# Two-layer hybrid decoder step: all feed-forward-in blocks by seven half-size products, even tiles first

## The chip, the cores and the metric

One Trainium2 chip, one core of it. The metric is the device time of one execution of the whole program in microseconds (us), as the median over the runs.

## The reference, cut to what matters

```python
def trunk_layer(x, pos, lw, states, front_pad, chunk, attend):
    m, new_states = hybrid_mixer(rmsnorm(x, lw['g_pre_mix']), ...)   # [...] @ lw['w_out'] at its end
    x = x + rmsnorm(m, lw['g_post_mix'])
    gate, up = jnp.split(rmsnorm(x, lw['g_pre_ffn']) @ lw['w_ffn_in'], 2, axis=-1)
    x = x + rmsnorm((jax.nn.silu(gate) * up) @ lw['w_ffn_out'], lw['g_post_ffn'])
    return x, new_states
```

There are two layers, 1104 tokens (9 token tiles: 8 of 128 and tile 8 of 80), a model width of 1024 and a feed-forward width of 2816. All data is float32.

## The kernel before, in words

Every float32 operand of a large product is split into two float16 halves (high and low), and a product is three float16 matmuls (high by high, high by low, low by high). Weights come from HBM as float32 into one of two `raw` buffers, ScalarE (ACT) writes the high half, VectorE (DVE) the low half; this is a split, and its result is a slab `wsp` in one of three `w` slots, three `w2` slots, or a `big` buffer.

The body is a set of Python generators, among which a planner (class `Plan`, line 116) picks the next by its own clocks; what it picks sets the order of the instructions on each engine, and each engine works through its own queue in that order. The places that matter here all lie in `dense` and what it starts:

- **Output projection** (lines 934 to 969). For each token tile i, two matmul groups (`hf`) of 24 matmuls of 512 columns into a PSUM bank `pd` (two banks take turns), evicted into `m`. For tiles 6 to 8 (`part`) seven of the eight contraction steps were done earlier and stored in `od`; here 3 matmuls per half are left, and DVE adds them to the loaded `m`. Tile i needs the outputs of the token mixers for tile i, the last of which is the delta-rule chain of head 3.
- **The norms of a tile** (`out_post`, line 2034, with `post_norm` and `norm_t`): a sum of squares on ACT, a scale and a power on GpSimd (POOL), a multiply with the gain and an add on DVE, a second sum of squares, scale, power and multiply, then eight 128x128 transposes on TensorE (PE) through the banks `ps_tr` and `ps_ch`, and their split into `xn2`. `xn2` keeps even tiles in its first half of columns and odd tiles in the second; tile 8 lies half in each.
- **Feed-forward in** (lines 973 to 1069), 22 column blocks c. Blocks 0 to 2 (`NPL`) are plain: gate and up for all 1104 tokens, first the columns of tiles 0 to 3 for all three blocks (k = 0), then the rest (k = 1). Blocks 3 to 21 are a Strassen scheme: tokens, contraction and gate/up are halved, and seven products of 24 matmul pairs of 256 and 296 columns replace the eight half-size products of a plain block.
- **The operands of the seven products** (`combos`, line 791): products 1 and 2 read the even half of `xn2` (a11, a12); products 5, 6 and 3 read sums `st`, product 7 a sum that overwrites a21 in `xn2`. Per group q of two tiles DVE, POOL and ACT work out the sums; `S1` marks `st`, `S3` the overwrite. The overwrite waits for the end of the plain blocks. DVE and POOL share the two-operand elementwise work by `tt` (line 308).
- **Weight loads** (`order_loads`, line 702; `loader`, `load7`): the queue order is the order of `want`. A Strassen block takes two loads of 512 KB and makes four slabs from 7 splits of 512 columns, with four sums on DVE or POOL.

Of the kernel before, what the change touches and what calls it, by code (L numbers as in the profile page):

```python
# [30 lines left out]
HS = 0.5 * DS * DS * XS  # L31
NPL = 3
NPT = 3
# [251 lines left out]
def build(tc, A, depth=DEPTH):  # L285
# [129 lines left out]
    def load7(my, key, src):  # L415
# [50 lines left out]
    def loader():  # L466
        while True:
# [13 lines left out]
            if spare:  # L481
                yield room(1)
                hold()
                raw = big([128, 1024], F32, "rawg")[:, :n]
                dma(raw, src)
            elif src is not None:
                wfree["raw"] -= 1
                raw = rawp.tile([128, 1024], F32, tag="raw", name="raw")[:, :n]
                dma(raw, src)
            if key[0] == "w2" and key[2] == 0:  # L490
# [211 lines left out]
    def order_loads(L):  # L702
# [87 lines left out]

    def combos(L, it, own):

# [38 lines left out]
        for q in own:  # L831
            f, g = temps(q)
            a11, a21 = part(xv[0, 0], q), part(xv[1, 0], q)
            yield (("S1", l, q),)
            tt(g, a11[:, :, 1], a21[:, :, 1], SUB)
            tt(f, a11[:, :, 0], a21[:, :, 0], SUB)
            tt(f, f, g, ADD)
            yield None
            put(a21, f)
            mark(("S3", l, q))  # L840
            yield None
        free()


    def dense():
        for L in LY[:depth]:
# [92 lines left out]
            mark(("gains", l))  # L939
            for i in range(NT):  # L940
                C = tsz(i)
# [6 lines left out]
                if not L.first:  # L948
# [22 lines left out]
            P.add(0, when([("xn2", l, i) for i in range(NT)], lambda: free(2)))  # L971

            yield (("ffn", l),)
            for k, c in [(k, c) for k in range(2) for c in range(NPL)]:
                wk = [("wi", l, c, z) for z in range(2)]
                if k == 0 and c % 2 == 0:
                    yield room(2)
                    hold(2)
                    hid_new(L)
                for h in range(2):  # L980
                    yield tuple(wk) + tuple(("xn2", l, i) for i in (4 * k + h, 4 * k + h + 2, 8 * k))
                    g0, gn = h * HT + CH[k][0], CH[k][1]
                    pgu = []
                    for gu in range(2):
                        p = pd(True)[:, :gn]
                        pgu.append(p)
                        for kt in range(8):
                            o = gu * 512 + kt % 4 * 128
                            w = slab[wk[kt // 4]][0]
                            mm3(p, w[:, 0, o:o + 128], w[:, 1, o:o + 128], L.xn2[:, kt, 0, g0:g0 + gn],  # L990
                                L.xn2[:, kt, 1, g0:g0 + gn], kt == 0, kt == 7)
                            yield NOW
                    a = abp.tile([128, 384], F32, tag="a", name="a")[:, :gn]
                    act(a, pgu[0], AF.Tanh, scale=DS * 0.5)
                    stt(a, a, 1.0, pgu[0], ADD, MUL)
                    for o, c0, cn in hid_out(L, c, h, k):
                        stt(o, a[:, c0:c0 + cn], HS, pgu[1][:, c0:c0 + cn], MUL, MUL)
                    yield NOW
                if k:
                    for w in wk:  # L1000
                        drop(w)
                    mark(("hid", l, c))
                if c == NPL - 1:
                    mark(("plain", l, k))

            yield room(1)
            hold()
            U = big([128, 2, HT], F32, "U")
            xv = L.xn2.rearrange("p (b k) z (s c) -> s b p k z c", b=2, s=2)
            ops = {1: xv[0, 0], 2: xv[0, 1], 3: L.st[:, 2], 4: xv[1, 1], 5: L.st[:, 0], 6: L.st[:, 1], 7: xv[1, 0]}  # L1010
            turn = 0
            for c in range(NPL, NF):
                if c % 2 == 0:
                    yield room(2)
                    hold(2)
                    hid_new(L)
                for n, (sl, o) in ((1, (0, 0)), (2, (0, 1)), (6, (1, 0)), (5, (1, 1)), (7, (2, 0)), (3, (2, 1)),
                                   (4, (3, 0))):
                    yield (("wi", l, c, sl),) + tuple(({6: "S1", 7: "S3"}[n], l, q) for q in range(5) if n > 5)
# [3 lines left out]
                    turn += 1  # L1023
                    for kt in range(4):
                        wh, wl = (w[:, z * 512 + kt * 128:z * 512 + kt * 128 + 128] for z in range(2))
                        x = ops[n][:, kt]
                        for z in range(2):
                            for q, (c0, cn) in zip(p, CH):
                                T.matmul(q[:, :cn], lhsT=wh, rhs=x[:, z, c0:c0 + cn], start=kt + z == 0, stop=False)
                        for q, (c0, cn) in zip(p, CH):  # L1030
                            T.matmul(q[:, :cn], lhsT=wl, rhs=x[:, 0, c0:c0 + cn], start=False, stop=kt == 3)
                        if kt < 3:
                            yield NOW
                    if o or sl == 3:
                        drop(("wi", l, c, sl))
                    for k, (q, (c0, cn)) in enumerate(zip(p, CH)):
# [1110 lines left out]
    for L in LY[:depth]:  # L2147
# [147 lines left out]
```

## Time and profile before

| | |
|---|---|
| median of 3 runs | 2858.16 us (2857.57 to 2859.92) |
| the profiled execution's own time | 2859.83 us |
| its span in the profile | 2858.0 us |
| PE busy in the span | 2730.1 us (96%) |
| DVE, ACT, POOL busy | 1938.0, 1287.5, 820.8 us |
| granted TensorE clock, mean | 0.984 |

Busy time of an engine is the sum of its instructions; PE is busy nearly all the time, so what counts is where it is not, and what it does there. A row of the timeline gives an instruction's start, its length, its engine, what it writes and reads, and in brackets how long its engine had been idle and which engine released it. Times are us from the span's start; layer 0's output projection and feed-forward-in begin at some 670, layer 1's at some 2083.

### The profile page before, as it was taken

The numbers are of one execution on the slowest core, as the hardware profiler recorded it, in microseconds if no ns is written. First come the engines' busy times: TensorE is split into PE (matmuls) and PEld (weight loads), VectorE is DVE, ScalarE is ACT, GpSimd is POOL, SyncE is SP. The second block draws the span as 40 slices with busy tenths as digits, with TensorE's granted clock in tenths as the row PEclk, the third lists the DMA queues.
The fourth block names the chain that finished last, engine by engine and source line by source line (L and its number), as shares of the span: only waits on it lengthen the run. The fifth ranks groups of instructions, "written<-read, shape, count | busy, mean of one in ns | idle before, by whom it ended". The sixth has DMA issues, their size and how long they took to land. (4 is left out here: it accounts for less than half of the span.)

```text
span 2858.0 us, 50012 instructions
## 1 busy us (share of the span) xinstructions
PE 2730.1 (96%) x19662; PEld 1907.6 (67%) x19662; DVE 1938.0 (68%) x3614; ACT 1287.5 (45%) x3015; POOL 820.8 (29%) x1124
## 2 busy tenths in 40 slices
PE   7999998999799999999999999999988999999998
PEld 4767676764588888744458676776646888887443
DVE  6467667655757776768875776666457667676778
ACT  5435456654423333433544455655543333333344
POOL 3205423313543333200260062233136232331002
PEclk9999999999899999999999999999999999999999
DMA  5011100132301111233340211001222111113324
GB/s 194 29 63 47 48 31 32 39 106 90 110 31 60 53 53 60 93 115 99 123 153 19 65 48 47 30 33 50 94 97 95 45 59 46 60 53 104 114 100 149
DMA packets 74092, 209.79 MB, mean 73 GB/s; under 512 B 13360, under 2 KB 24816, under 8 KB 73824
## 3 DMA queue, kind: packets, MB, share of 16 engines
q1 hardware_dynamic: 73856, 206.59, 22.0%
q8 instruction: 154, 2.52, 0.4%
q14 instruction: 82, 0.67, 0.1%
HBM read 175.49 MB, written 33.04 MB: 73 GB/s over the span
## 5 line engine op out<-in xcount | busy, mean ns | idle before, releaser
L215 PEld LDWEIGHTS <-wsp 128*128 128x128 f16 x10704 | 1044.4, 99 | 306.3 <-issue 14.6
L215 PE MATMUL pd<-xn,wsp 128*128 128x336 f16 (+3 forms) x4512 | 740.7, 311 | 3.4 <-DVE a L215 3.2
L215 DVE SCALAR_TENSOR_TENSOR wsp<-raw,wsp 128x512 f16<-128x512 f32 (+2 forms) x390 | 377.4, 977 | 184.1 <-ACT wsp L215 181.3
L215 ACT ACTIVATE wsp<-raw 128x512 f16<-128x512 f32 (+2 forms) x390 | 287.4, 749 | 367.3 <-DVE raw L215 106.5
L215 PEld LDWEIGHTS <-hsp 128*128 128x128 f16 x1848 | 180.9, 98 | 222.9 <-DVE hsp L215 4.3
L215 PE MATMUL pd<-wsp,hsp 128*128 128x512 f16 x924 | 224.5, 381 | 3.8 <-DVE hsp L215 1.9
L215 PE MATMUL ps_o<-wsp,hsp 128*128 128x512 f16 x924 | 222.5, 379 | 0.0
L215 PE MATMUL pd<-wsp,mixed 128*128 128x512 f16 (+1 forms) x864 | 212.6, 385 | 7.3 <-DVE m L215 7.3
L215 POOL TENSOR_SCALAR rqy<-ss 128x1 f32<-128x1 f32 (+1 forms) x72 | 65.5, 910 | 528.1 <-ACT jk L215 390.9
L215 DVE SCALAR_TENSOR_TENSOR u<-R,lp_cw,u 128x512 f32<-128x512 f32 x216 | 180.3, 870 | 11.3 <-ACT u L215 10.3
L215 ACT ACTIVATE hsp<-hid 128x512 f16<-128x512 f32 x154 | 89.9, 619 | 176.4 <-PE ps_o L215 143.8
L215 POOL TENSOR_TENSOR raw<-raw 128x512 f32<-128x512 f32 x74 | 95.6, 1293 | 241.9 <-DVE raw L215 212.6
L215 PE MATMUL ps_o<-xn,wsp 128*128 128x256 f16 (+1 forms) x1296 | 163.7, 284 | 0.0
L215 PE MATMUL pd<-wsp,xn 128*128 128x512 f16 (+3 forms) x864 | 156.0, 331 | 3.5 <-ACT wsp L215 1.7
L215 PE MATMUL ps_inv<-xn,wsp 128*128 128x256 f16 (+1 forms) x1248 | 154.0, 281 | 0.8 <-DVE a L215 0.8
L215 POOL TENSOR_TENSOR U<-U,hid 128x256 f32<-128x256 f32 (+1 forms) x114 | 80.3, 732 | 239.4 <-ACT hid L215 239.4
L215 PEld LDWEIGHTS <-mixed 128*128 128x128 f16 (+1 forms) x864 | 84.6, 101 | 84.3 <-issue 13.6
L215 DVE TENSOR_TENSOR hsp<-hid,hsp 128x512 f16<-128x512 f32 x154 | 101.2, 684 | 40.8 <-ACT hsp L215 40.8
L215 PEld LDWEIGHTS <-xn 128*128 128x128 f16 (+1 forms) x864 | 86.3, 101 | 51.1 <-issue 3.3
L215 PE MATMUL ps_ch<-xn,wsp 128*128 128x296 f16 x456 | 109.2, 289 | 0.0
L215 PE MATMUL ps_tr<-xn,wsp 128*128 128x256 f16 x456 | 108.6, 273 | 0.0
L215 DVE TENSOR_TENSOR W<-ps_inv,c 128x512 f16<-128x512 f32 (+1 forms) x120 | 71.0, 595 | 47.8 <-PE ps_inv L215 46.9
(498 smaller groups left out, 4790.9 us busy)
## 6 DMA issues: line engine op xcount, KB each, us to landing
raw<-wfi SPq DMA_DIRECT2D x88, 512.0 KB, 3.5
raw<-wfo SPq DMA_DIRECT2D x50, 512.0 KB, 3.6
raw<-wf SPq DMA_DIRECT2D x44, 512.0 KB, 3.3
xd<-xt SPq DMA_DIRECT2D x24, 512.0 KB, 2.9
xt<-xd SPq DMA_DIRECT2D x24, 512.0 KB, 4.7
rawg<-wfo SPq DMA_DIRECT2D x20, 512.0 KB, 4.3
xt<-x SPq DMA_DIRECT2D x16, 512.0 KB, 4.6
raw<-wo SPq DMA_DIRECT2D x16, 512.0 KB, 3.4
```

The source lines that it names most:

```text
L215: r = f(*a, **kw)
```

## The change

- `NPL` goes. All 22 blocks take the seven products. For the first four (`NPRE`) products 1 and 2 are done ahead of everything else (the "pre" products), as they read the even half alone, and are kept in the block's output buffers `hid`; after these the remaining five products of blocks 0 to 3 follow, then blocks 4 to 21 as before.
- The pre products have weights of their own: four loads `wj` of 512 KB, each a slab of 1024 columns. Blocks 0 to 3 load their full weights again afterwards, and leave out two of the seven splits.
- Output projection goes through the tiles in the order 0, 6, 8, 2, 4, 7, 1, 3, 5 (`OUT_SEQ`).
- `combos` takes the groups in the order 4, 3, 0, 1, 2, marks `S1` after the two sums that products 5 and 6 read, and does the other two at once, without a wait for plain blocks.

```diff
-NPL = 3
+NPRE = 4
+OUT_SEQ = (0, 6, 8, 2, 4, 7, 1, 3, 5)
...
         for k in range(4):
+            if k == 0 and key[2] < NPRE:
+                yield lambda: split[0] == my
+                tt(a, b, a, SUB)
+                continue
...
+        for c in range(NPRE):
+            want(("wj", l, c), A["wfi"][l, 2 * c:2 * c + 2, :, 0:4, :].rearrange("z p a b -> p z (a b)"), 1024, "f")
         for c in range(NF):
-            src = [A["wfi"][l, 2 * c + z].rearrange("p a b -> p (a b)") for z in range(2)]
-            if c < NPL:
-                for z in range(2):
-                    want(("wi", l, c, z), src[z], 1024, "f")
-            else:
-                want(("wi", l, c), src, 1024, "s")
+            want(("wi", l, c), [A["wfi"][l, 2 * c + z].rearrange("p a b -> p (a b)") for z in range(2)], 1024, "s")
...
-            tt(f, a12[:, :, 0], g, SUB)
-            tt(f, f, a12[:, :, 1], ADD)
-            yield None
-            put(part(L.st[:, 2], q), f)
             mark(("S1", l, q))
             yield None
-        if NPL:
-            yield (("plain", l, 0), ("plain", l, 1))
...
+            for o, a in ((a21, a22), (part(L.st[:, 2], q), a12)):
+                tt(f, a[:, :, 0], g, SUB)
+                tt(f, f, a[:, :, 1], ADD)
+                yield None
+                put(o, f)
+                yield None
             mark(("S3", l, q))
...
-            for i in range(NT):
+            for i in OUT_SEQ:
...
-            for k, c in [(k, c) for k in range(2) for c in range(NPL)]:
...
+            for c in range(NPRE):
...
+                for n in range(2):
+                    yield (("wj", l, c),) + tuple(("xn2", l, i) for i in (0, 2, 4, 6, 8))
+                    p = [pd(True) for _ in range(2)]
+                    yield from half(p, slab[("wj", l, c)][0].rearrange("p z a -> p (z a)"), n * 512, 1024, xv[0, n])
+                    for k, (q, (c0, cn)) in enumerate(zip(p, CH)):
+                        b1 = hid_out(L, c, 0, k)[0][0]
+                        for o, o0, on in hid_out(L, c, 1, k):
+                            if n == 0:
+                                act(o, q[:, o0:o0 + on])
+                            else:
+                                V.tensor_tensor(b1[:, o0:o0 + on], q[:, o0:o0 + on], o, op=ADD)
+                        if n:
+                            gate(b1, cn)
+                    yield NOW
+                drop(("wj", l, c))
...
-            for c in range(NPL, NF):
+            for c in range(NF):
...
-                                   (4, (3, 0))):
+                                   (4, (3, 0)))[0 if c >= NPRE else 2:]:
...
-        it = iter(range(5))
-        P.add(2, combos(L, it, (0, 2, 4)))
-        P.add(2, combos(L, it, (1, 3)))
+        it = iter((4, 3, 0, 1, 2))
+        P.add(2, combos(L, it))
+        P.add(2, combos(L, it))
```

Three places in layer 0 show how the instructions move. In the names below `m2_` and `xt_` are one tile's rows in output projection and its norms, `wsp_` a slab, `raw_` its loaded weights, `rqy_` what POOL's power gives, `pd_` a PSUM bank.

The first is DVE at the start of output projection, when tile 0's products are done (tile 0 is `m2_7804`). Before:

```order
L215 TENSOR_TENSOR m2_7804<-m2_7804,gpo_7466 128x1024
L215 SCALAR_TENSOR_TENSOR mixed_7594<-g__7788,nwd_355,mixed_7594 128x80
L215 SCALAR_TENSOR_TENSOR xt_7805<-m2_7804,rqy_7880,xt_7805 128x1024
L215 SCALAR_TENSOR_TENSOR wsp_7807<-raw_7073,wsp_7807 128x1024
L215 SCALAR_TENSOR_TENSOR wsp_7812<-raw_7155,wsp_7812 128x1024
L215 SCALAR_TENSOR_TENSOR m2_7804<-xt_7805,rqy_7887,gpf_7468 128x1024
```

With the change (tile 6 is `m2_7874`, tile 8 `m2_7916`):

```order
L216 TENSOR_TENSOR m2_7804<-m2_7804,gpo_7466 128x1024
L216 SCALAR_TENSOR_TENSOR m2_7874<-pd_7911,m2_7874 128x512
L216 SCALAR_TENSOR_TENSOR wsp_7807<-raw_7073,wsp_7807 128x1024
L216 SCALAR_TENSOR_TENSOR wsp_7812<-raw_7155,wsp_7812 128x1024
L216 SCALAR_TENSOR_TENSOR xt_7805<-m2_7804,rqy_7881,xt_7805 128x1024
L216 SCALAR_TENSOR_TENSOR xt_7876<-m2_7874,rqy_7923,xt_7876 128x1024
L216 SCALAR_TENSOR_TENSOR m2_7916<-pd_7927,m2_7916 80x512
L216 SCALAR_TENSOR_TENSOR m2_7804<-xt_7805,rqy_7888,gpf_7468 128x1024
L216 SCALAR_TENSOR_TENSOR m2_7916<-pd_7932,m2_7916 80x512
```

Before, nothing but tile 0's norm and two splits stands here. Now the two evictions of tile 8's banks (`pd_7927`, `pd_7932`) stand behind tile 6's `xt_7876`, which reads `rqy_7923` from POOL.

The second is ACT where the sums of a group q are written (`st`, and `xn` from `tm`). Before, with the eviction of tile 3's second bank (`pd_8086`):

```order
L215 ACTIVATE st_7801<-tm_7802 128x4x128
L215 ACTIVATE xn_7470,ss_8112<-xt_7958 128x16x64
L215 ACTIVATE m2_8043<-pd_8046 128x512
L215 ACTIVATE st_7801<-tm_7802 128x4x128
L215 ACTIVATE m2_8043<-pd_8086 128x512
```

With the change, with the eviction of tile 4's second bank (`pd_8066`):

```order
L216 ACTIVATE xn_7470<-ps_ch_8077 128x4x2x40
L216 ACTIVATE st_7801<-tm_7802 128x4x40 x2
L216 ACTIVATE xn_7470<-tm_7802 128x4x40
L216 ACTIVATE xn_7470<-ps_tr_8103 128x4x128
L216 ACTIVATE xn_7470<-ps_ch_8110 128x4x128
L216 ACTIVATE st_7801<-tm_7802 128x4x40
L216 ACTIVATE m2_8020<-pd_8066 128x512
```

The eviction of `pd_8066` now stands behind three writes of group 4's sums and the two of tile 2's transposes; before, one write of sums stood between the two evictions of a tile.

The third is DVE around the end of output projection. Before (tile 4 is `m2_8118`, tile 5 `m2_8222`, tiles 6 and 7 `m2_8317` and `m2_8342`):

```order
L215 SCALAR_TENSOR_TENSOR xt_8119<-m2_8118,rqy_8244,xt_8119 128x1024
L215 SCALAR_TENSOR_TENSOR wsp_8448<-raw_7815,wsp_8448 128x1024
L215 SCALAR_TENSOR_TENSOR wsp_8482<-raw_7865,wsp_8482 128x1024
L215 SCALAR_TENSOR_TENSOR m2_8118<-xt_8119,rqy_8287,gpf_7468 128x1024
L215 TENSOR_TENSOR xn_7470<-ps_tr_8301,xn_7470 128x4x128
L215 TENSOR_TENSOR xn_7470<-ps_ch_8308,xn_7470 128x4x128
L215 SCALAR_TENSOR_TENSOR m2_8317<-pd_8332,m2_8317 128x512
L215 SCALAR_TENSOR_TENSOR m2_8317<-pd_8337,m2_8317 128x512
L215 SCALAR_TENSOR_TENSOR xt_8223<-m2_8222,rqy_8322,xt_8223 128x1024
```

With the change (tile 3 is `m2_8254`, tile 5, now the last, `m2_8363`):

```order
L216 SCALAR_TENSOR_TENSOR xt_8255<-m2_8254,rqy_8387,xt_8255 128x1024
L216 TENSOR_TENSOR tm_7802<-tm_7802,xn_7470 128x512
L216 SCALAR_TENSOR_TENSOR wsp_8457<-raw_7815,wsp_8457 128x1024
L216 SCALAR_TENSOR_TENSOR wsp_8526<-raw_7865,wsp_8526 128x512
L216 TENSOR_TENSOR xn_7470<-tm_7802,xn_7470 128x4x128
L216 SCALAR_TENSOR_TENSOR m2_8254<-xt_8255,rqy_8452,gpf_7468 128x1024
L216 TENSOR_TENSOR tm_7802<-tm_7802,xn_7470 128x512
L216 TENSOR_TENSOR raw_8460<-raw_8460,raw_7865 128x512
L216 SCALAR_TENSOR_TENSOR wsp_8526<-raw_7865,wsp_8526 128x512
L216 TENSOR_TENSOR m2_8363<-m2_8363,gpo_7466 128x1024
L216 SCALAR_TENSOR_TENSOR wsp_8654<-raw_8460,wsp_8654 128x512
L216 SCALAR_TENSOR_TENSOR xt_8364<-m2_8363,rqy_8480,xt_8364 128x1024
```

Now the split of the last `wj` (`wsp_8457`), two of block 0's splits and a sum on `raw_8460` stand ahead of tile 5's `xt_8364`. `raw_8460` is loaded into the buffer that `raw_7815` leaves once `wsp_8457` is split.

## Rows read from the trace of the kernel before

**Rows 1.** The page: span and busy time of each engine.

```profile
PE 2730.1 (96%) x19662; PEld 1907.6 (67%) x19662; DVE 1938.0 (68%) x3614; ACT 1287.5 (45%) x3015; POOL 820.8 (29%) x1124
```

**Rows 2.** Busy time by stretch: start:end, length, engines (instructions), clock, DMA share, GB/s.

```profile
672.09:749.20 77.11, 65.20 (x312) 32.26 (x313) 46.60 (x49) 34.27 (x59) 32.83 (x36) 0.95 0.37 125
749.20:829.93 80.73, 74.35 (x595) 60.82 (x593) 52.18 (x75) 25.74 (x53) 41.53 (x40) 0.92 0.16 52
829.93:1200.00 370.07, 369.96 (x3149) 307.85 (x3148) 257.95 (x523) 133.44 (x301) 114.86 (x148) 1.00 0.17 55
2084.67:2162.90 78.23, 65.10 (x313) 32.17 (x314) 46.91 (x50) 35.47 (x61) 33.81 (x38) 0.95 0.37 127
2162.90:2242.68 79.78, 72.39 (x594) 59.66 (x593) 52.80 (x74) 25.02 (x51) 39.87 (x38) 0.94 0.14 48
```

**Rows 3.** Timeline of PE, layer 0: projection, plain blocks, seven products (start, length).

```profile
681.35 10.52 PE L215 MATMUL pd<-wsp,mixed 128*128 128x512 f16 x48
...
780.31 5.40 PE L215 MATMUL ps_o<-xn,wsp 128*128 128x256 f16 x48
785.55 5.40 PE L215 MATMUL ps_inv<-xn,wsp 128*128 128x256 f16 x48
...
802.47 6.20 PE L215 MATMUL ps_inv<-xn,wsp 128*128 128x296 f16 x48
808.51 6.20 PE L215 MATMUL pd<-xn,wsp 128*128 128x296 f16 x48
...
832.75 2.98 PE L215 MATMUL ps_inv<-xn,wsp 128*128 128x256 f16 x24
835.57 2.98 PE L215 MATMUL ps_o<-st,wsp 128*128 128x256 f16 x24
```

**Rows 4.** Timeline of PE, layer 0: rows ahead of which it stood idle.

```profile
680.45 0.63 PE L215 MATMUL ps_tr<-c,m 128*128 128x128 f32 x4 [1.50 <-DVE m L215]
...
718.65 1.09 PE L215 MATMUL ps_tr<-c,m 128*128 128x128 f32 x4 [3.08 <-DVE m L215]
...
737.58 0.63 PE L215 MATMUL ps_tr<-c,m 128*128 128x128 f32 x4 [2.27 <-DVE m L215]
...
747.80 1.83 PE L215 MATMUL pd<-wsp,mixed 128*80 128x512 f16 x6 [2.92 <-DVE m L215]
...
773.40 1.08 PE L215 MATMUL ps_tr<-c,m 128*128 128x128 f32 x4 [2.86 <-DVE m L215]
```

**Rows 5.** Timeline, layer 0: the norms of tile 0, from its eviction on.

```profile
670.99 0.60 ACT L215 ACTIVATE m<-pd 128x512 f32<-128x512 f32 x1
...
671.62 1.06 ACT L215 ACTIVATE xn<-m 128x1024 f16<-128x1024 f32 x1
...
674.74 1.28 DVE L215 SCALAR_TENSOR_TENSOR xt<-m,rqy,xt 128x1024 f32<-128x1024 f32 x1 [0.50 <-POOL rqy L215]
675.94 2.35 DVE L215 SCALAR_TENSOR_TENSOR wsp<-raw,wsp 128x1024 f16<-128x1024 f32 x2
...
677.36 0.99 POOL L215 TENSOR_SCALAR rqy<-ss 128x1 f32<-128x1 f32 x1 [2.65 <-ACT xn L215]
...
679.01 1.29 DVE L215 SCALAR_TENSOR_TENSOR m<-xt,rqy,gpf 128x1024 f32<-128x1024 f32 x1 [0.72 <-POOL rqy L215]
```

**Rows 6.** Timeline, layer 0: DVE and POOL at once.

```profile
743.71 2.35 POOL L215 TENSOR_TENSOR m<-m,gpo 128x1024 f32<-128x1024 f32 x1
743.79 3.36 DVE L215 SCALAR_TENSOR_TENSOR xt<-m,rqy,xt 128x1024 f32<-128x1024 f32 x1 [1.83 <-POOL rqy L215]
```

**Rows 7.** Groups by form, 665 to 860: count | busy, mean ns | idle before.

```profile
L215 DVE SCALAR_TENSOR_TENSOR wsp<-raw,wsp 128x512 f16<-128x512 f32 x19 | 14.5, 774 | 9.4 <-ACT wsp L215 9.4
...
L215 DVE TENSOR_TENSOR tm<-tm,xn 128x512 f32<-128x512 f32 x8 | 7.8, 973 | 5.6 <-POOL tm L215 5.6
...
L215 POOL TENSOR_TENSOR tm<-tm,xn 128x512 f32<-128x512 f32 x4 | 5.0, 1240 | 1.0 <-DVE tm L215 0.8
...
L215 POOL TENSOR_TENSOR tm<-xn 128x160 f32<-128x160 f16 x3 | 1.8, 609 | 1.4 <-ACT xn L215 1.3
```

**Rows 8.** The page: weight loads, KB each, us from issue to landing.

```profile
raw<-wfi SPq DMA_DIRECT2D x88, 512.0 KB, 3.5
```

More of the change, by code (lines that the diff above doesn't have):

```diff
@@ L488, in loader @@
                 raw = rawp.tile([128, 1024], F32, tag="raw", name="raw")[:, :n]
-                dma(raw, src)
+                dma(raw.rearrange("p (z a) -> p z a", z=2) if key[0] == "wj" else raw, src)
             if key[0] == "w2" and key[2] == 0:
@@ L789, in hid_tails, with combos @@
             yield None
-    def combos(L, it, own):
+    def combos(L, it):
         l = L.l
@@ L804, in part @@
             return x[:, :, :, q * 128:min(q * 128 + 128, HT)]
-        def temps(q):
+        for q in it:
             n = 128 if q < 4 else 40
-            return (tm[:, t, :4 * n].rearrange("p (k c) -> p k c", k=4) for t in range(2))
-        for q in it:
-            f, g = temps(q)
+            f, g = (tm[:, t, :4 * n].rearrange("p (k c) -> p k c", k=4) for t in range(2))
             a11, a12, a21, a22 = (part(xv[s, b], q) for s in range(2) for b in range(2))
@@ L822, in combos @@
             put(part(L.st[:, 1], q), g)
-            tt(f, a12[:, :, 0], g, SUB)
-            tt(f, f, a12[:, :, 1], ADD)
-            yield None
-            put(part(L.st[:, 2], q), f)
             mark(("S1", l, q))
             yield None
-        if NPL:
-            yield (("plain", l, 0), ("plain", l, 1))
[L831 to L839, printed above, removed]
+            for o, a in ((a21, a22), (part(L.st[:, 2], q), a12)):
[4 more added lines that the diff above has]
+                yield None
             mark(("S3", l, q))
-            yield None
         free()
@@ L973, in dense @@
             yield (("ffn", l),)
-            for k, c in [(k, c) for k in range(2) for c in range(NPL)]:
[L975 to L1004, printed above, removed]
@@ L1006, in dense, with half @@
-            yield room(1)
-            hold()
-            U = big([128, 2, HT], F32, "U")
-            xv = L.xn2.rearrange("p (b k) z (s c) -> s b p k z c", b=2, s=2)
-            ops = {1: xv[0, 0], 2: xv[0, 1], 3: L.st[:, 2], 4: xv[1, 1], 5: L.st[:, 0], 6: L.st[:, 1], 7: xv[1, 0]}
-            turn = 0
-            for c in range(NPL, NF):
+            xv = L.xn2.rearrange("p (b k) z (s c) -> s b p k z c", b=2, s=2)
+            def half(p, w, o, w2, x):
+                for kt in range(4):
+                    wh, wl = (w[:, z * w2 + o + kt * 128:z * w2 + o + kt * 128 + 128] for z in range(2))
+                    for z in range(2):
+                        for q, (c0, cn) in zip(p, CH):
+                            T.matmul(q[:, :cn], lhsT=wh, rhs=x[:, kt, z, c0:c0 + cn], start=kt + z == 0, stop=False)
+                    for q, (c0, cn) in zip(p, CH):
+                        T.matmul(q[:, :cn], lhsT=wl, rhs=x[:, kt, 0, c0:c0 + cn], start=False, stop=kt == 3)
+                    if kt < 3:
+                        yield NOW
@@ L1013, in dense, with gate @@
+            def gate(b1, cn):
+                a = abp.tile([128, 384], F32, tag="a", name="a")[:, :cn]
+                act(a, b1, AF.Tanh, scale=DS * 0.5)
+                stt(b1, a, 1.0, b1, ADD, MUL)
+            for c in range(NPRE):
                 if c % 2 == 0:
@@ L1016, in dense @@
                     hid_new(L)
+                for n in range(2):
[11 more added lines that the diff above has]
+                            gate(b1, cn)
+                    yield NOW
+                drop(("wj", l, c))
+            yield room(1)
+            hold()
+            U = big([128, 2, HT], F32, "U")
+            ops = {1: xv[0, 0], 2: xv[0, 1], 3: L.st[:, 2], 4: xv[1, 1], 5: L.st[:, 0], 6: L.st[:, 1], 7: xv[1, 0]}
+            turn = 0
+            for c in range(NF):
+                if c >= NPRE and c % 2 == 0:
+                    yield room(2)
+                    hold(2)
+                    hid_new(L)
                 for n, (sl, o) in ((1, (0, 0)), (2, (0, 1)), (6, (1, 0)), (5, (1, 1)), (7, (2, 0)), (3, (2, 1)),
-                                   (4, (3, 0))):
+                                   (4, (3, 0)))[0 if c >= NPRE else 2:]:
                     yield (("wi", l, c, sl),) + tuple(({6: "S1", 7: "S3"}[n], l, q) for q in range(5) if n > 5)
@@ L1023, in dense @@
                     turn += 1
[L1024 to L1033, printed above, removed]
+                    yield from half(p, w, 0, 512, ops[n])
                     if o or sl == 3:
@@ L1043, in dense @@
                             V.tensor_tensor(b1, q, ua, op=ADD)
-                            a = abp.tile([128, 384], F32, tag="a", name="a")[:, :cn]
-                            act(a, b1, AF.Tanh, scale=DS * 0.5)
-                            stt(b1, a, 1.0, b1, ADD, MUL)
+                            gate(b1, cn)
+                        elif n == 6 and c < NPRE:
+                            for o, o0, on in b2:
+                                V.tensor_tensor(ua[:, o0:o0 + on], q[:, o0:o0 + on], o, op=ADD)
                         elif n == 6:
```

2 lines of the change are left out of this document (1 added, 1 removed).

## The prediction, as it was made before the run

> **What bounds the kernel now.** I read the page first: PE is busy 96% of the span [rows 1], so only work taken off PE, or its waits, can change the time. Then the stretches [rows 2]. In the seven-product stretch from 829.93 PE is busy 369.96 of 370.07 us at a granted clock of 1.00, the higher of its two levels: nothing is to be had there but less work. The other four stretches are output projection and the plain blocks, once per layer (77.11 and 80.73 us in layer 0, 78.23 and 79.78 in layer 1); there PE waits, and the clock is 0.92 to 0.95. Last the timeline of PE there: what it waits for is a transpose of a tile's normed rows, or a bank that DVE has not emptied, for 1.5 to 3.1 us at a time [rows 4].
>
> What PE's work costs at the full clock [rows 3]: a row's length includes a modelled tail (rows 5.40 long follow each other after 5.24). 48 projection matmuls of 10.52 less that tail are 0.215 each. A plain block is two rows of 5.24 and two of 6.04, 22.56 us. A product is 2.82 us, seven are 19.74. A tile's transposes are 0.9 (680.45 to 681.35, [rows 3, 4]).
>
> So the losses now: layer 0's first stretch of 77.11 [rows 2] holds 253 projection matmuls (54.4), five tiles' transposes (4.5) and 32 plain matmuls at 0.109 (3.5), which leaves **14.7** for waits and low clock. The second, 80.73, holds the rest of three plain blocks (67.7 - 3.5) and four tiles' transposes (3.6), which leaves **12.9**. Layer 1 gives 15.8 and 12.0 in the same way.
>
> **The change, part by part.** *Removed:* three plain blocks per layer become Strassen blocks, 3 x (22.56 - 19.74) = **8.5 us per layer** off PE, all of it on the path since PE ends last. That is sure.
>
> *Loads and splits:* 48 weight loads of 512 KB per layer for 44, and 154 splits of 512 columns for 145. A load takes 3.5 us [rows 8] and the DMA engines are 17% busy in the long stretch [rows 2]; nine splits are 9 x 0.77 of DVE [rows 7], which is 70% busy there (257.95 of 370.07 [rows 2]). In the five-product rounds of blocks 0 to 3, DVE's 13.75 us per block fall by two splits and the first two products' evictions, some 3, in 14.1 us: 76%. PE covers both; I cost them at nothing. Were that cover gone, each split that is late would hold a product by at most its own 0.77.
>
> *Output projection in the new order.* Before, tiles 1 to 5, 10.3 us of PE each, stood between tile 0 and the cheap tiles 6 to 8, whose halves are three matmuls (0.65). Now tiles 6 and 8 come straight behind tile 0, so PE has 3 us of work where it had 10 while tile 0 goes through its norms. I follow the queues in layer 0's clock.
>
> (1) Tiles 6 and 8 need the last outputs of the delta-rule chain, which ends only then, and a bank each; no row shows this wait. The nearest is the 2.92 for tile 8's bank at 747.80 [rows 4]; bounds 0 and 6, taken 3.0.
>
> (2) PE runs dry at about 676.6. Tile 2 needs the bank of tile 8, whose eviction on DVE stands behind two splits (2.35 [rows 5], to 678.2), tile 0's `xt_7805` and tile 6's `xt_7876`. POOL's multiply of tile 6 by the gain (2.35, about 677.2 to 679.55) runs meanwhile, and a DVE operation that meets it ends 1.1 after it: the row of 3.36 where 1.28 is usual [rows 5, 6]. So `xt_7805` ends at 680.65, `xt_7876` at 681.95, the eviction at 682.6: a wait of 6. Tile 0's second sum of squares and POOL's 1.6 then let its transposes go at 685.1, two matmuls later: 2 more. Before, that place cost 1.50 [rows 4]. Bounds 4 and 10; taken 8.0.
>
> (3) Tile 7's second half needs the bank of tile 4's second half, whose eviction on ACT stands behind group 4's chain of some ten small operations on three engines (0.6 each on POOL [rows 7]) that starts only once tile 8 is transposed and split: 4.9. If the chain is twice as fast, nothing; if twice as slow, 11.
>
> (4) Tile 1's transposes: its norms meet the group of tiles 6 and 7 on POOL and DVE. 5.1, against 3.08 for the worst such wait now [rows 4]; bounds 1 and 7.
>
> With 0.2 for tile 2 these are 21.2, and for the clock I take 4, as now (0.95 over 77.11 is 3.9 [rows 2]). 25.2 for 14.7: **+10.5 per layer**.
>
> *After projection.* Eight pre products are 22.6 us of PE, where the plain blocks were 67.7. Under them must go the norms of tiles 3 and 5, the sums of groups 1 and 2, and block 0's weights. The last `wj` is split only when projection's own slabs leave their slots, and DVE gets to it about 1 us after projection's last matmul; the load of `raw_8460` is issued behind it, and behind the store of tile 3 on SP's queue, and lands 3.5 to 4 later [rows 8]. DVE and POOL then do their sums on it ahead of tile 5's `xt_8364` and its power. With 1.2 to 1.3 per operation that meets the other engine [rows 7], tile 3's transposes come 4.8 and tile 5's 19.5 after projection's end; PE is there at 2.8 and 11.3: waits of 2.0 and 8.2, plus 3 of low clock, 13.2 for 12.9: **+0.3**. What is late next is product 6, whose operand needs tile 5: that is ready some 17 us after tile 5's transposes, when the rest of the pre products, 14 to 16 us, has just ended; POOL's last write for product 7 comes before product 5 ends. I cost both at nothing; if group 2's sums come later, each us is one us of PE.
>
> **Sum.** -8.5 + 10.5 + 0.3 = +2.3 per layer, +4.6 in all. On the profiled execution's own 2859.8 that is 2864.4; it lies 1.7 above the median, so the forecast is **2863 us**, a change inside what a measurement of this kernel can tell from none (0.2%, 5.7 us).
>
> **The rivals.** *No longer waits than now.* If the queues slip past each other so that the two stretches lose 27.6 per layer as they do now, the 17 us off PE all show: 2858 - 17 = 2841; half of it, 2850. For it: in (2) to (4) one early power or one early sum dissolves the wait, and what is lost there also gives DVE time to catch up. Against: PE's cover behind tile 0 and behind projection is gone, by count of matmuls. Chance 0.25.
>
> *DVE and POOL block each other.* Between tile 3's norms and tile 5's transposes POOL has twelve 512-column operations of 1.24 [rows 7], where PE now waits for DVE. My sum lets DVE sit out about five of them; sitting out all adds 7 x 1.2 = 8.4 per layer, 2863 + 17 = 2880. It decides from 0.5 us per layer on, since 2863 is 1 us below the bound: less than half of one such operation more. For it: the 3.36 [rows 6]. Against: DVE's mean on such operands is 0.97 [rows 7], less than one POOL operation, so most do not sit one out whole. The Trainium skill ("SBUF — State Buffer", Who interferes with whom) says that a VectorE instruction with two SBUF inputs and a GpSimd one that reads SBUF hold the shared port for their whole length, the later one fully blocked. By that rule the rival's 2880 comes out rather than 2863; the row of 3.36 agrees with it, 2.27 left of POOL's 2.35 and then 1.09. Chance 0.26.
>
> *The five-product rounds starve.* A round has 14.1 us of PE for five splits, their sums and the evictions, just as DVE is late from the pre products. At 1 us per round, eight rounds: 2871. For it: DVE's 76%. Against: 24% to spare, and two blocks' loads ahead. Chance 0.10.
>
> **How the numbers follow.** The forecast keeps 0.39. Its own range, with (1) to (4) and the two late waits each a fifth off in the same direction, is 2863 +- 10. The range for eight in ten reaches half-way to the first rival and nearly to the second: 2848 to 2879. Faster by over 0.2%: the first rival, 0.25. Slower: the second and third, 0.36. Same: 0.39.
>
> **What would show it.** Right: the rows of PE after tile 0 show 5 to 9 us of idle before tile 2's second pair of matmuls and tile 0's transposes, released by DVE; idle before tile 7's second half, released by ACT; and 6 to 10 us before tile 5's transposes amid the pre products. Product 6 of block 0 then starts within 2 us of the pre products' end. From there on blocks take 14.1 and 19.74 without idle. Wrong: a wait of over 3 us before product 6 or 7 (second rival), PE below 98% busy in the five-product rounds (third), or no wait over 4 us in output projection (first).

## The result, and the profile after

The changed kernel takes **2875.97 us** (median of 4 runs, 2873.03 to 2879.61) where the kernel before took 2858.36 beside it (4 runs): a ratio of 1.0062, 95% interval 1.0044 to 1.0079. That is 17.6 us slower. The forecast was 2863, no change that can be told; the result lies near the upper end of the range and beside the second rival's 2880.

The page of the changed kernel, whose span is 2876.0 us, to be held against [rows 1]:

```profile
PE 2721.0 (95%) x19518; PEld 1895.5 (66%) x19518; DVE 1995.5 (69%) x3720; ACT 1306.4 (45%) x3075; POOL 862.0 (30%) x1166
```

PE has less to do and the span is longer, so waits and low clock have more than eaten what was removed. Where, the stretches of layer 0 show (columns as in [rows 2]):

```profile
672.09:754.10 82.01, 66.31 (x308) 32.81 (x309) 55.36 (x62) 36.78 (x67) 43.11 (x49) 0.90 0.36 121
754.10:775.30 21.20, 12.58 (x106) 10.12 (x103) 18.78 (x24) 11.38 (x25) 14.68 (x13) 0.92 0.21 75
775.30:789.00 13.70, 13.66 (x104) 11.34 (x104) 13.70 (x16) 4.81 (x11) 9.40 (x7) 0.88 0.24 78
789.00:797.10 8.10, 0.71 (x5) 0.17 (x3) 5.98 (x8) 3.82 (x9) 8.02 (x7) 0.70 0.00 0
797.10:803.00 5.90, 5.90 (x29) 3.93 (x29) 5.77 (x11) 2.01 (x6) 1.27 (x2) 0.54 0.27 89
803.00:829.93 26.93, 26.93 (x232) 22.42 (x230) 22.67 (x45) 8.83 (x21) 12.05 (x15) 1.00 0.21 63
829.93:1200.00 370.07, 370.07 (x3152) 308.19 (x3150) 258.91 (x532) 132.45 (x299) 116.81 (x150) 1.00 0.18 56
```

The first row is output projection to its last matmul at about 754.1, the second and third the eight pre products. From 803.00 on PE is busy all the time, as before. New is the fourth row: 8.1 us in which PE works 0.71, while POOL is busy 8.02. In the fifth PE is busy all the time at a granted clock of 0.54 and gets 29 matmuls done, where 53 fit into the same 5.90 us at 1.00 (a row of the run without sums, below).

The timeline of PE names the waits; these rows answer to [rows 4]. The last two are layer 1's:

```profile
672.12 0.81 PE L216 MATMUL pd<-wsp,mixed 128*80 128x512 f16 x3 [0.50 <-DVE m L216]
674.08 0.81 PE L216 MATMUL pd<-wsp,mixed 128*80 128x512 f16 x3 [1.15 <-DVE m L216]
682.23 1.01 PE L216 MATMUL pd<-wsp,mixed 128*128 128x512 f16 x2 [7.34 <-DVE m L216]
712.40 12.51 PE L216 MATMUL pd<-wsp,mixed 128*128 128x512 f16 x48 [2.81 <-ACT m L216]
738.34 1.09 PE L216 MATMUL ps_tr<-c,m 128*128 128x128 f32 x4 [3.74 <-DVE m L216]
758.13 0.63 PE L216 MATMUL ps_tr<-c,m 128*128 128x128 f32 x4 [0.98 <-DVE m L216]
775.34 1.09 PE L216 MATMUL ps_tr<-c,m 128*128 128x128 f32 x4 [7.68 <-DVE m L216]
792.53 0.39 PE L216 MATMUL pd<-st,wsp 128*128 128x256 f16 x1 [3.25 <-DVE hid L216]
797.06 3.17 PE L216 MATMUL pd<-st,wsp 128*128 128x296 f16 x13 [4.14 <-ACT hid L216]
...
2219.18 1.01 PE L216 MATMUL pd<-st,wsp 128*128 128x256 f16 x4 [7.61 <-ACT hid L216]
2223.06 3.90 PE L216 MATMUL pd<-st,wsp 128*128 128x296 f16 x20 [2.87 <-DVE hid L216]
```

Everything down to 775.34 was named ahead, in its place and about its size. The 7.4 us at 792.53 and 797.06 (10.5 in layer 1) were not: they stand before product 6 of block 0. What ends them is not the operand `st` but `hid`, that is, evictions that empty the banks of the last pre products. What kept DVE and ACT from them is in the timeline of DVE, POOL and ACT, same place:

```profile
785.37 1.65 DVE L216 TENSOR_TENSOR tm<-tm,xn 128x512 f32<-128x512 f32 x1
...
786.54 1.48 POOL L216 TENSOR_TENSOR tm<-tm,xn 128x512 f32<-128x512 f32 x1
786.94 1.64 DVE L216 TENSOR_TENSOR raw<-raw 128x512 f32<-128x512 f32 x1
787.99 1.60 POOL L216 TENSOR_TENSOR st<-tm,st 128x512 f16<-128x512 f32 x1
...
788.50 1.64 DVE L216 SCALAR_TENSOR_TENSOR wsp<-raw,wsp 128x512 f16<-128x512 f32 x1
789.55 1.60 POOL L216 TENSOR_TENSOR tm<-tm,xn 128x512 f32<-128x512 f32 x1
790.06 1.64 DVE L216 TENSOR_TENSOR st<-tm,st 128x512 f16<-128x512 f32 x1
...
792.39 0.88 DVE L216 TENSOR_TENSOR st<-tm,st 128x512 f16<-128x512 f32 x1
...
792.68 1.72 POOL L216 TENSOR_TENSOR raw<-raw 128x512 f32<-128x512 f32 x1
...
794.42 0.63 ACT L216 ACTIVATE wsp<-raw 128x512 f16<-128x512 f32 x1 [2.09 <-POOL raw L216]
...
796.12 0.61 ACT L216 ACTIVATE wsp<-raw 128x512 f16<-128x512 f32 x1
796.64 0.36 ACT L216 ACTIVATE hid<-pd 128x256 f32<-128x256 f32 x1
...
799.35 0.68 DVE L216 TENSOR_TENSOR tm<-xn,tm 128x512 f32<-128x512 f16 x1
799.95 0.68 DVE L216 SCALAR_TENSOR_TENSOR wsp<-raw,wsp 128x512 f16<-128x512 f32 x1
800.55 0.68 DVE L216 TENSOR_TENSOR tm<-tm,xn 128x512 f32<-128x512 f32 x1
```

Two things are to be seen. First, DVE and POOL take turns: each DVE row is 1.64 long and ends some 0.56 after the POOL row that began before it (786.54 + 1.48 = 788.02, and 786.94 + 1.64 = 788.58), and the next POOL row in its turn ends 1.0 after DVE's. One operation of each is done every 1.56 us. With POOL idle, from 799.35, DVE starts an operation of the same size every 0.60. Both engines together do two in the time in which DVE alone does two and a half. Second, ACT's eviction at 796.64 stands behind block 0's weight splits, one of which waited 2.09 for POOL's subtraction `raw`. So the banks were late because evictions, splits and sums stand in the same queues; the runs below take these apart.

### The profile page after: what moved, and what is told of

It is laid out like the page before. It is cut to its first block, busy times and chain, and to the rows that moved or that the text cites. A ratio compares the mean times of both kernels' runs of the same rounds, so it can differ in the third digit from the quotient of the medians.

```text
span 2876.0 us, 49982 instructions
## 1 busy us (share of the span) xinstructions
PE 2721.0 (95%) x19518; PEld 1895.5 (66%) x19518; DVE 1995.5 (69%) x3720; ACT 1306.4 (45%) x3075; POOL 862.0 (30%) x1166
## 3 DMA queue, kind: packets, MB, share of 16 engines
q1 hardware_dynamic: 76032, 210.79, 22.6%
## 5 line engine op out<-in xcount | busy, mean ns | idle before, releaser
L216 PEld LDWEIGHTS <-wsp 128*128 128x128 f16 x10560 | 1031.6, 99 | 323.4 <-issue 30.8
L216 PE MATMUL pd<-xn,wsp 128*128 128x384 f16 (+3 forms) x4308 | 729.5, 312 | 1.7 <-ACT m L216 1.7
L216 DVE SCALAR_TENSOR_TENSOR wsp<-raw,wsp 128x512 f16<-128x512 f32 (+2 forms) x412 | 403.7, 989 | 177.5 <-ACT wsp L216 175.0
L216 ACT ACTIVATE wsp<-raw 128x512 f16<-128x512 f32 (+2 forms) x412 | 299.3, 738 | 376.6 <-DVE raw L216 116.1
L216 PE MATMUL pd<-wsp,mixed 128*128 128x512 f16 (+1 forms) x864 | 215.2, 385 | 22.6 <-DVE m L216 18.0
L216 POOL TENSOR_TENSOR raw<-raw 128x512 f32<-128x512 f32 x86 | 112.1, 1304 | 252.2 <-DVE raw L216 238.7
L216 POOL TENSOR_TENSOR U<-U,hid 128x256 f32<-128x256 f32 x132 | 93.6, 738 | 271.5 <-ACT hid L216 271.5
L216 PE MATMUL ps_inv<-xn,wsp 128*128 128x296 f16 (+1 forms) x1080 | 148.0, 281 | 0.9 <-ACT xn L216 0.9
L216 PE MATMUL ps_o<-xn,wsp 128*128 128x296 f16 (+1 forms) x1044 | 147.9, 284 | 0.0
L216 PE MATMUL pd<-st,wsp 128*128 128x296 f16 (+1 forms) x768 | 100.3, 289 | 17.9 <-ACT hid L216 11.8
L216 PE MATMUL ps_ch<-xn,wsp 128*128 128x296 f16 x480 | 115.0, 289 | 0.0
```

Of the source, the lines that this page charges most:

```text
L216: r = f(*a, **kw)
```

## The experiments

Every run was timed over several rounds beside the kernel before on its chip; the table orders them by what they showed. A difference is the run's median less that of the kernel before.

| run | what differs | us | difference | ratio, 95% interval |
|---|---|---|---|---|
| the change | | 2875.97 | +17.6 | 1.0062 (1.0044 to 1.0079) |
| old_order | old order of tiles | 2912.16 | +55.9 | 1.0195 (1.0181 to 1.0209) |
| tile2_second | tile 2 ahead of 6 and 8 | 2872.34 | +15.3 | 1.0059 (1.0047 to 1.0072) |
| banks_apart | product 6 in other banks | 2868.72 | +12.5 | 1.0046 (1.0034 to 1.0059) |
| sums_left_out | no token sums | 2828.93 | -27.3 | 0.9908 (0.9894 to 0.9921) |
| eight_ahead | 16 pre products | 2860.51 | +3.5 | 1.0011 (1.0002 to 1.0020) |
| sums_on_dve | sums on DVE alone | 2857.42 | +0.4 | 1.0000 (0.9991 to 1.0008) |
| sums_splits_on_dve | also two blocks' subtractions | 2850.31 | -6.7 | 0.9975 (0.9966 to 0.9984) |
| all_on_dve | also the multiply by the gain | 2837.78 | -17.9 | 0.9937 (0.9925 to 0.9950) |
| all_on_dve_eight_ahead | both | 2825.11 | -30.6 | 0.9894 (0.9879 to 0.9910) |
| order_alone | plain blocks, new order | 2847.87 | -8.4 | 0.9969 (0.9958 to 0.9981) |
| plain_sums_on_dve | the same, sums on DVE | 2841.00 | -14.7 | 0.9945 (0.9932 to 0.9957) |
| plain_all_on_dve | the same, multiply on DVE | 2840.14 | -16.7 | 0.9945 (0.9931 to 0.9958) |

**Which part costs.** The change has two parts, the order and the products; each was run without the other.

```diff
-OUT_SEQ = (0, 6, 8, 2, 4, 7, 1, 3, 5)
+OUT_SEQ = tuple(range(9))
```

> The changed kernel with output projection's tiles in the old order 0 to 8, all else kept. Theory A (most of the +17.6 us is the wait before product 6 of block 0, 7.4 us of idle PE and some 2.5 of low clock per layer, because the last pre products' banks and group 2's sums are late on DVE, POOL and ACT): the order's own 6.7 us per layer in projection go, but the first pre product then waits for tile 8, the last tile, with nothing to cover its norms (8 or more per layer), so 2870 to 2882 us. Theory B (the order is what costs): 2876 - 2 x 6.7 = 2862 or less.

The old order is much worse, +55.9: theory B has the wrong sign, and theory A is right in that but 30 us short. In its timeline of PE the wait for the last tile's transposes, with no matmuls left to cover it, is there, and the wait before product 6 is larger than in the changed kernel (9.22 for 7.39):

```profile
758.80 1.09 PE L216 MATMUL ps_tr<-c,m 128*128 128x128 f32 x4 [9.49 <-DVE m L216]
...
796.62 0.37 PE L216 MATMUL pd<-st,wsp 128*128 128x256 f16 x1 [9.22 <-ACT st L216]
```

Behind it PE waits for `st` again and again, 1.74, 2.25 and 1.90 the longest; the 30 us are not accounted for in full.

The other way round, the kernel before with the new order alone:

```diff
-            for i in range(NT):
+            for i in OUT_SEQ:
...
-                       + tuple(wo if i == 0 else ()))
+                       + tuple(wo if i == OUT_SEQ[0] else ()))
```

> The kernel before with only the order of output projection changed; its plain blocks stay. Theory A: projection loses the 6.7 us per layer that it lost in the changed kernel (idle of about 7.3 before tile 2's second matmuls), and the plain blocks, 67.7 us of PE behind it, cover tiles 3 and 5 and all sums, so nothing is added after it: 2862 to 2872. Theory B: the same 13 us and the late norms as well, 2872 to 2880. If the order costs nothing: 2858.

Neither theory had this: the order by itself is 8.4 us **faster**, with the very wait in projection that the prediction charged to it. Its timeline of PE:

```profile
681.03 1.01 PE L216 MATMUL pd<-wsp,mixed 128*128 128x512 f16 x2 [7.34 <-DVE m L216]
...
756.52 5.06 PE L216 MATMUL ps_o<-xn,wsp 128*128 128x256 f16 x23 [2.84 <-DVE xn L216]
```

After 756.52 it does not wait for a tile or a sum again; the plain blocks cover the late norms, where the kernel before still waits for tile 5 at 773.40 [rows 4]. I read the gain there and have not tested it further. So the products are what costs: 17.6 + 8.4 = 26 us more than plain blocks in the same order, though PE has 17 us less of matmuls with them.

**Banks or sums.** Product 6 was given the transposes' banks, which are free by then.

```diff
-            turn = 0
+            turn = 3
```

> The changed kernel with the rotation of PSUM banks for the products begun at the transposes' two banks (turn = 3), so that product 6 of block 0 needs no bank of a pre product; product 5 needs them 2.8 us later. Theory A1 (the banks, held by evictions that stand behind splits and sums on ACT and DVE, set product 6's start): its 3.25 + 4.14 us of idle in layer 0 shrink to some 2.4 for group 2's sums and 2 before product 5, so 2868 to 2872. Theory A2 (group 2's sums set it): within 3 us of 2876.

2868.7, as A1 has it. In its timeline of PE the releaser before product 6 has changed from `hid` to `st`, group 2's sums, and 7.4 us of idle have become 3.6:

```profile
791.45 0.41 PE L216 MATMUL ps_ch<-st,wsp 128*128 128x296 f16 x1 [2.76 <-ACT st L216]
...
792.90 0.41 PE L216 MATMUL ps_ch<-st,wsp 128*128 128x296 f16 x1 [0.83 <-DVE st L216]
```

The banks were the later of the two, by 3.8 us of idle in layer 0, but not all of it: behind them the sums are late, in the same queues. The intervals of this run and of the change overlap; the step rests on the rows.

**The sums themselves.** This run leaves out the sums: the loop over the groups only waits for its tiles and marks them done, and products 3, 5, 6 and 7 read parts of `xn2` as they stand.

```diff
-            tt(g, a21[:, :, 1], a22[:, :, 1], ADD)
...
+            mark(("S1", l, q), ("S3", l, q))
...
-            ops = {1: xv[0, 0], 2: xv[0, 1], 3: L.st[:, 2], 4: xv[1, 1], 5: L.st[:, 0], 6: L.st[:, 1], 7: xv[1, 0]}
+            ops = {1: xv[0, 0], 2: xv[0, 1], 3: xv[0, 0], 4: xv[1, 1], 5: xv[0, 1], 6: xv[1, 1], 7: xv[1, 0]}
```

> The changed kernel without the token sums and differences of groups 0 to 4 (products 3, 5, 6 and 7 read parts of xn2 as it stands, so what they give is not the block's). Theory A: DVE and POOL are free of some 14 operations between tile 3's norms and product 6, the wait of 7.4 us and the low clock behind it go, and tile 5's transposes come 3 to 5 us sooner: 2876 - 2 x (10 to 14) = 2848 to 2856. Theory C (the late load and splits of block 0's own weights hold product 6): 2866 or more.

2828.9: theory C's late load falls, since nothing was done to the loads; the splits come sooner too, as DVE and POOL are free for them. Theory A is right in kind and has some half of the size: 22 us per layer go, not 10 to 14. Product 6 does not wait, tile 5's transposes wait 0.59 for 7.68, and the clock stays up. Its timeline row for tile 5 and its stretches in the place where the changed kernel stands still:

```profile
761.74 0.64 PE L216 MATMUL ps_tr<-c,m 128*128 128x128 f32 x4 [0.59 <-DVE m L216]
```

```profile
789.00:797.10 8.10, 8.10 (x72) 6.75 (x70) 5.96 (x17) 2.43 (x6) 1.92 (x4) 1.00 0.38 129
797.10:803.00 5.90, 5.90 (x53) 4.92 (x51) 5.06 (x7) 1.98 (x6) 5.62 (x6) 1.00 0.00 0
```

**Sharing the work, or doing it on one engine.** The sums were left in and taken off POOL: in `combos` every `tt`, which picks the engine by the planner's cost, became an operation of DVE.

```diff
-            tt(g, a21[:, :, 1], a22[:, :, 1], ADD)
+            V.tensor_tensor(g, a21[:, :, 1], a22[:, :, 1], op=ADD)
```

> The changed kernel with every operation of the token sums on DVE, none on POOL (the sums are the same). In the changed kernel 23 sums of 512 columns stood on POOL at 1.2 to 1.8 us each from 671 to 806 us, and 24 on DVE, 0.68 alone but 1.64 beside POOL. Theory A, the engines' blocking counts: all 47 on DVE are 32 us for the 25 that DVE's 24 take now, but every chain of four sums shrinks from some 6 to some 3.5 us, so tile 5's transposes and product 6 come 3 to 5 us sooner per layer: 2863 to 2870. Rival D, DVE's own load counts: 7 us more on DVE per layer before product 6, so 2880 to 2892.

17 us are won, more than theory A said, by giving the busier engine all of the work: rival D falls. The timeline of PE and ACT shows where. The wait before tile 5's transposes falls from 7.68 to 1.25. Product 6 still waits, 1.05 and 4.57, now for ACT's write of `st`, and that stands behind a split that waited 3.35 for POOL's `raw`:

```profile
762.08 0.63 PE L216 MATMUL ps_tr<-c,m 128*128 128x128 f32 x4 [1.25 <-DVE m L216]
...
779.88 0.63 ACT L216 ACTIVATE wsp<-raw 128x512 f16<-128x512 f32 x1 [3.35 <-POOL raw L216]
780.41 0.61 ACT L216 ACTIVATE st<-tm 128x512 f16<-128x512 f32 x1
...
781.08 1.26 PE L216 MATMUL pd<-st,wsp 128*128 128x296 f16 x5 [4.57 <-ACT st L216]
```

Then the same for the subtractions of blocks 0 and 1:

```diff
+        t7 = tt if key[2] > 1 else lambda o, x, y, op: V.tensor_tensor(o, x, y, op=op)
...
-                tt(a, b, a, SUB)
+                t7(a, b, a, SUB)
```

> The same, and the subtractions of the weights of blocks 0 and 1 on DVE too, so that ACT's splits and evictions never wait for POOL in the last pre products. Theory A: ACT's eviction for product 6's second bank no longer stands behind a split that waits for POOL (2.1 us), another 2 to 3 us per layer: 2858 to 2866. Rival D: 5 more operations of 0.8 on DVE: 2884 to 2898.

2850.3, another 7 us and again below the range, now 0.25% faster than the kernel before. DVE and POOL blocking each other goes, as the groups by form from 671 to 806 us show. First the changed kernel, then this run:

```profile
L216 DVE SCALAR_TENSOR_TENSOR wsp<-raw,wsp 128x512 f16<-128x512 f32 x10 | 10.7, 1074 | 0.0
...
L216 DVE TENSOR_TENSOR tm<-tm,xn 128x512 f32<-128x512 f32 x10 | 8.7, 875 | 2.1 <-POOL tm L216 2.1
...
L216 DVE TENSOR_TENSOR raw<-raw 128x512 f32<-128x512 f32 x4 | 5.7, 1426 | 1.2 <-POOL raw L216 1.2
```

```profile
L216 DVE TENSOR_TENSOR tm<-tm,xn 128x512 f32<-128x512 f32 x16 | 10.7, 682 | 0.0
...
L216 DVE SCALAR_TENSOR_TENSOR wsp<-raw,wsp 128x512 f16<-128x512 f32 x11 | 7.6, 692 | 0.0
L216 DVE TENSOR_TENSOR raw<-raw 128x512 f32<-128x512 f32 x9 | 7.0, 799 | 2.8 <-POOL raw L216 2.8
```

36 such operations of DVE take 25.3 us here, where 24 took 25.1: the twelve more cost nothing, since DVE is hardly held up any more. How much of the 17 and the 7 us is the blocking these runs don't separate from two other gains: a chain of sums no longer passes from engine to engine, and POOL by itself is slower (with DVE idle it takes 1.15 us for a sum of 512 columns, at 794.36 in the changed kernel; DVE starts one every 0.60).

Last the multiply by the gain in `post_norm`:

```diff
-        tt(m[:C], m[:C], gb[:C], MUL)
+        V.tensor_tensor(m[:C], m[:C], gb[:C], op=MUL)
```

> sums_splits_on_dve, and the multiply by the gain after the mixing norm on DVE too (POOL took it for tile 6 and some others), so that POOL has only the small norm operations. In the changed kernel that multiply took 3.21 us on POOL and the operation on DVE beside it 3.36 for 1.28. Step (2) of the prediction: the 7.34 of idle before tile 2's second matmuls falls by 2.1 less 1.2 for the multiply itself on DVE, and tile 8's by as much: 2 x (1 to 3) below 2850, 2844 to 2848. If DVE's queue is the limit there: 2850 to 2856.

2837.8, more won than expected. The `xt` operation that was 3.36 in the changed kernel is 1.27, and the wait before tile 2's second matmuls is 4.39 for 7.34 (timeline of DVE and PE):

```profile
676.96 1.27 DVE L216 SCALAR_TENSOR_TENSOR xt<-m,rqy,xt 128x1024 f32<-128x1024 f32 x1
...
680.03 1.01 PE L216 MATMUL pd<-wsp,mixed 128*128 128x512 f16 x2 [4.39 <-DVE m L216]
```

**More cover.** Cover is what PE has to do while something else is late. Here the sums are on both engines as in the change, but twice the pre products stand ahead of them:

```diff
-NPRE = 4
+NPRE = 8
```

> The changed kernel with eight blocks' first two products ahead (NPRE = 8) for four: 45.1 us of PE for 22.6 between output projection and product 6, four loads more per layer. Theory E (the cover is what the change took away): product 6's waits of 7.4 us and the low clock behind them go, tile 5's transposes still come late but PE has other products before them: 2876 - 2 x (9 to 16) = 2844 to 2858. If the pre products' weights come late instead (each needs a split of two 512-column halves in a slot that the pre product before it frees): 2862 or more.

14 us better than the change, just above theory E's 2844 to 2858 and below the other's 2862. The wait before product 6 goes. Tile 5's transposes still wait, and PE stops between pre products for banks (timeline of PE):

```profile
770.79 1.09 PE L216 MATMUL ps_tr<-c,m 128*128 128x128 f32 x4 [6.48 <-DVE m L216]
...
793.00 0.27 PE L216 MATMUL pd<-xn,wsp 128*128 128x256 f16 x1 [2.11 <-ACT hid L216]
```

With everything on DVE as well:

> all_on_dve with eight blocks' first two products ahead. If cover and blocking are two remedies for one wait (product 6 and tile 5 late), the second adds little: 2840 to 2850. If what is left is DVE's own work under too few products (waits of 1 to 3 us in blocks 0 to 3 of sums_splits_on_dve), 22.6 us more of pre products take these too: 2830 to 2840.

2825.1, below both ranges, **1.06% faster than the kernel before** and the best of all. Cover and blocking are not two remedies for one wait; their gains nearly add (14.1 and 35.5 against the change, 48.2 together).

**Another order.** Tile 2 second, to cover tile 0's norms:

```diff
-OUT_SEQ = (0, 6, 8, 2, 4, 7, 1, 3, 5)
+OUT_SEQ = (0, 2, 6, 8, 4, 7, 1, 3, 5)
```

> The changed kernel with tile 2 ahead of tiles 6 and 8 in output projection: (0, 2, 6, 8, 4, 7, 1, 3, 5). Tile 2's 10.3 us of PE cover tile 0's norms, so the idle of 7.34 before tile 2's second matmuls goes; tiles 6 and 8 then stand behind tile 2 and their banks wait for its eviction on ACT and tile 0's norms on DVE, 2 to 4. Step (2) of the prediction right: 4 to 6 us per layer are won, 2864 to 2868. If the wait only moves behind tile 8: 2872 to 2878.

2872.3 on a chip on which the kernel before took 2857.1: the interval overlaps that of the change. The wait has moved behind tile 8, 6.67 for 7.34, and product 6 waits as it did, 6.12 for ACT's `hid` (timeline of PE):

```profile
689.16 1.01 PE L216 MATMUL pd<-wsp,mixed 128*128 128x512 f16 x2 [6.67 <-DVE m L216]
```

**The same remedies with plain blocks.** Their edits are those shown, made in order_alone.

> The kernel before (plain blocks) in the new order, as in order_alone, with its token sums on DVE alone. Theory A (blocking costs where PE has little to do meanwhile): with 67.7 us of plain blocks behind projection the sums are covered on either engine, so within 4 us of order_alone's 2848. If POOL's sums are simply slow work that the kernel waits for anywhere, the 18 us that sums_on_dve won return here: 2830 to 2838.

2841.0, between the two. The sums on DVE bring 6.3 us where plain blocks cover them and 17.2 where they don't: most of the cost is in the lack of cover, not all of it.

> plain_sums_on_dve with the multiply by the gain on DVE too: the plain blocks with every remedy that all_on_dve has. all_on_dve_eight_ahead (2825) against it says what the seven products bring once their cover is back. If the 17.0 us of matmuls removed show in full: 2842 or more. If the multiply wins here what it won there (12.5 of 2850 to 2838, 2.9 of it per layer in the wait before tile 2): 2829 to 2837, and the seven products bring 4 to 12 of their 17.

2840.1, between the two: the multiply brings 2 us here for the 11 it brought to the seven products, and the intervals can't tell 2 from nothing. With this the products can be priced in four settings, always against plain blocks in the same order (the subtractions of blocks 0 and 1, on DVE in the last two rows, exist with the products alone):

| setting | plain blocks | seven products | the products' part |
|---|---|---|---|
| as in the change | -8.4 | +17.6 | +26.0 |
| sums on DVE | -14.7 | +0.4 | +15.1 |
| all on DVE | -16.7 | -17.9 | -1.2 |
| all on DVE, eight ahead | -16.7 | -30.6 | -13.9 |

The -1.2 lies inside the intervals, the others outside. The 17.0 us of matmuls were there to be had all along, and 13.9 of them show once the work around them has cover and one engine.

## Why the prediction was right in its range and wrong in a step

2876 lies inside the range of 2848 to 2879, but the forecast was no change, and the kernel is slower: the whole interval lies above 1. Per layer the forecast was +2.3 and the trace shows +8.9 (one row of layer 1 that both kernels have, the transposes of `ye`, starts at 2079.69 before and 2088.62 after). By its steps, in layer 0:

- **Removed, 8.5.** Right: PE has 144 matmuls less (19518 for 19662), 24 for each of the six blocks, and that is one product (24 matmuls, 12 pairs of 256 and 296 columns). In the last setting of the table 13.9 of the 17.0 us show.
- **Output projection, steps (1) to (4).** Right in place and releaser, high in sum, 16.0 for 21.0: 1.65 for 3.0 (two waits), 7.34 and 0.48 for 6 and 2, 2.81 for 4.9, 3.74 for 5.1. Projection ends at 754.1 where the steps add up to 757.9, 3.8 better. The mechanism of (2), POOL's multiply against `xt_7805`, is shown by all_on_dve. What the steps left out is that the same order gives back more than it takes: order_alone is 8.4 us faster.
- **Loads, splits and the five-product rounds, nothing.** Right for the rounds: PE is busy 26.93 of 26.93 and 370.07 of 370.07 us, so nothing starves. The third rival falls. Ahead of the rounds the splits did cost, as the last point says.
- **Tiles 3 and 5.** Right: 0.98 for 2.0 and 7.68 for 8.2.
- **"Product 6 ... I cost both at nothing": this step failed.** It measured 10.1 us: 7.4 of idle, then 5.9 at a clock of 0.54 (29 matmuls where 53 fit, 24 x 0.11 = 2.7 lost). Its two times were right. The operand, "some 17" after tile 5's transposes, has its last write at 793.27, after 17.9 (the DVE row at 792.39; in banks_apart the same write releases product 6). The pre products, 14 to 16, ended after 13.9. But their difference, 1 to 3 by the prediction's own figures and 4.0 in the trace, was put at nothing; banks_apart, which waits for the operand alone, shows 3.6 of idle. The other 3.8 come from what was never looked at: product 6 needs two banks of the pre products, and their evictions on DVE and ACT stand behind sums and block 0's splits, which wait for POOL. The second bank is free only at 797.0. 10.1 more, less the 3.8 and 1.5 that projection, tile 3 and tile 5 came out better, is 4.8 of the 6.6 between +2.3 and +8.9; 1.8 of low clock and small waits I don't assign.

A slip in the sums beside it: (1) to (4) and the two late waits are 31.2 per layer, and a fifth of them over two layers is 12.5, not 10; and 2848 lies two thirds of the way to the first rival, not half.

The mechanism was the second rival's, and the sign named for it, a wait of over 3 us before product 6, came. Its time was close too, 2880 against 2876, but partly by luck. It looked for the blocking ahead of tile 5's transposes, and there the wait came out as the forecast had it, which had five blocked operations in its sum already; two DVE operations of 512 columns took 1.6 us or more between tile 3's transposes and tile 5's last norm operation, and eight from there to 791.70. The loss at product 6 and what other steps had too high came near the rival's 8.4 per layer together.

The argument held against it was that DVE's mean on such operands, 0.97 [rows 7], is less than one operation of POOL. That mean hides a mix. Of its eight operations seven took 0.68 to 0.87, and one, which met POOL's multiply, 2.82 (timeline of the kernel before, POOL and DVE):

```profile
759.17 2.34 POOL L215 TENSOR_TENSOR m<-m,gpo 80x1024 f32<-80x1024 f32 x1
759.25 2.82 DVE L215 TENSOR_TENSOR tm<-tm,xn 128x512 f32<-128x512 f32 x1 [0.67 <-POOL tm L215]
```

So a low mean says that few of them met POOL in the kernel before, not that a meeting is cheap. In the changed kernel, from 785.37 to 791.70 us, *all four* operations of DVE are ones of 1.64, and those of POOL beside them are 1.5 to 1.6. The rule that stood beside the rival, from the Trainium skill ("SBUF — State Buffer", Who interferes with whom), is what the trace shows there: the later of the two instructions waits for the whole of the earlier one, and 0.56 + 1.0 follow each other in every 1.56.

## What to carry to other kernels

Before a stretch of matmuls is shortened, ask what the stretch was covering: here 67.7 us of plain blocks hid most of five groups of sums, and 22.6 us of pre products did not. Work that DVE and POOL share is not halved where each holds the other up, and a mean over a group hides that; look for the longest rows of the group, and try it on one engine alone. When a product's operand has been timed, time its banks too: who evicts them, and behind what in that queue.

## What was not expected of the hardware

A DVE operation of 512 columns with two SBUF inputs starts every 0.60 us when POOL is idle; with POOL at work on SBUF too, a pair of one each takes 1.56, so a second engine made this work slower (0.78 for 0.60 an operation). DVE's evictions, which read a PSUM bank and one SBUF operand, were not held up: one of 256 columns took 0.41 at 791.62, beside a POOL operation, and 0.41 at 801.16, with POOL idle. With 36 operations in place of 24, DVE's busy time in three groups stayed as it was (25.3 for 25.1 us), and with sums, splits and multiply all on DVE the kernel lost 35.5 us.

PE was granted 0.54, near the lower of its two levels, for the 5.9 us after the 7.4 of idle, although it was busy all that time: a wait of 7.4 us cost some 10.
